# A hybrid attention and mLSTM model: the plain step's rotation in tiles of its own, and another order of the last pair's scores, exchange and weight splits

## The chip, the cores and the metric

The kernel runs on one core of a Trainium2 chip. The core has five engines: PE (TensorE, matmuls into PSUM), DVE (VectorE), ACT (ScalarE), POOL (GpSimd, here mostly a queue that issues DMAs) and SP (SyncE, a queue that issues DMAs). Each engine takes its instructions in order from its own queue, and waits on semaphores for the others. The metric is the device time of one execution in microseconds.

## The reference, cut to what matters

Two layers over a sequence of 512 tokens with 1024 features: dilated attention with a SwiGLU, then an mLSTM with a SwiGLU. The change lies in the attention layer alone.

```python
DIL_CONFIGS = ((128, 1), (512, 4), (2048, 16))     # 3 groups: window, dilation
ATTN_HEADS, ATTN_HEAD_DIM, ROT_DIM = 8, 128, 32

def dilated_attention_mixer(xn, positions, w_in, w_out):
    proj = (xn @ w_in).reshape(B, S, N_GROUPS, 3, ATTN_HEADS, ATTN_HEAD_DIM)
    scale = ATTN_HEAD_DIM ** -0.5
    for g, (window, dilation) in enumerate(DIL_CONFIGS):
        q = apply_partial_rope(proj[:, :, g, 0], positions) * scale   # rotates 32 of 128 features
        k = apply_partial_rope(proj[:, :, g, 1], positions)
        v = proj[:, :, g, 2]
        o, lse = dilated_window_attention(q, k, v, window, dilation)
        outs.append(o); lses.append(lse)
    wts = jax.nn.softmax(jnp.stack(lses), axis=0)                     # one softmax over the groups
    o = jnp.einsum('gbsh,gbshd->bshd', wts, jnp.stack(outs))
    return o.reshape(B, S, ATTN_WIDTH) @ w_out

def reference(...):
    h = x
    h = h + dilated_attention_mixer(rms_norm(h, attn_norm[0]), positions, attn_w_in[0], attn_w_out[0])
    h = h + swiglu(rms_norm(h, ffn_norm[0]), ffn_w_in[0], ffn_w_out[0])
    h = h + mlstm_mixer(rms_norm(h, mlstm_norm[0]), ...)
    h = h + swiglu(rms_norm(h, ffn_norm[1]), ffn_w_in[1], ffn_w_out[1])
    return rms_norm(h, final_norm)
```

## The kernel before

**Matmuls in three passes.** Every large operand is split in a high and a low part, and a product is made of three matmuls: high by high, high by low, low by high (`SPLITS`). A weight chunk of 128x1024 (or a block difference) is loaded on SP's queue into a `wraw` buffer, its high part is copied by ACT (L217) and its low part is subtracted by DVE (L219), both in `split_chunk`. A `Feed` makes the chunks in the order of a plan, two, later three, ahead of the one in use: what a chunk's preparation issues is traced three chunks before PE needs it. Activations are split the same way by `split_act` (L233 on ACT, L234 on DVE).

**Order of the work.** The program is traced once, and a compile-time planner then orders each engine's queue: of the instructions that its own timing has ready it takes the one traced first. An edge from `tc.issue_after(ins)` keeps an instruction behind `ins` on the same engine. `run` does this for PE on both sides, so that a piece of work stands as one block between two others. `defer(n, fn)` traces a piece of work n steps later, where `advance()` is called at the end of a step. `behind_scores` holds the low splits and the block differences behind `ahead_of_splits`, the last reduction of the latest plain scores.

**Attention, pair by pair.** The 8 heads are done in 4 pairs (`pr` 0 to 3), each in three groups `g`. In pairs 1 to 3 group 0 is the plain step (`project_pair` and `project`): query, then key, two chunks each, so four steps. Groups 1 and 2 are each a `qk_unit` of seven products of 24 matmuls in the order P1, P5, P6, P2, P7, P3, P4 (a Strassen-like scheme), with steps ending after P5, P2, P3 and P4. ACT copies partial sums out of PSUM (L885 after P1, L888 after P5, L890 after P6, L897 after P2 and P4). P7 goes on adding to the PSUM bank that L890 reads, so P7's first matmul waits for L890. P5 of the next group waits for a bank that L897 of P4 reads last.

**Rotation.** 32 of the 128 features of each query and key are packed into one tile of 128 partitions (`rot`, tag "rot", one buffer), by ACT (L965 in the plain step, L879 `pack` in the units). `rope` turns them on DVE (L598 to L607), and its `back` copies them back on ACT: 8 copies at L613 in the plain step, 4 at L615 in the units. The last unit (pair 3, group 2) adds straight into the query and key (L604). The plain step's `back` is deferred by one step, into the next unit, after its P5.

**Scores, softmax and values.** `scores0` does the plain group's scores (L691), masks and reduces them on DVE (L697) and takes exponentials on ACT (L732); it is deferred by 6 steps (`SCORES0_AT`) from the end of the plain step, so it stands in group 2 behind P2. `scores12` does groups 1 and 2 (L713, L716, L738), one step into the next pair. `joint` exchanges the maxima and sums between the groups' orders of the tokens (a matmul, L751) and makes the factors; `weigh` multiplies them in (L783, L786), `transposes` turns a head's weights over (L792) and stores them to memory with four DMAs on POOL (L795), `bring` loads them back (L800, on POOL, in the last pair on SP), and `values` multiplies by the values (L810, L815). `RUN_AT` holds the steps for all that: scores of groups 1 and 2, the rest (joint with the first head's weighing, its transposes, the second head's weighing, its transposes with the first load, the second load), the two heads' values, and the loads of the values. PSUM has two banks for each head's scores, "s" and "o", and the values use "o" too; `keep_head` (L627) copies a head's output out of it.

**After the last pair** follows a wide product of the values of groups 1 and 2 (`project_tokens_wide`, L331: four chunks of 24 matmuls, each in four blocks of tokens), with the last pair's scores after its first chunk and its joint work amid the third (`amid=(2, 1)`), all of it by `LAST_AT`. The heads kept in memory come back (`bring_heads`, L634), four of them are split (L233, L234), and the output projection begins (`out_part`, L249), with the last pair's values put between its parts.

Of the kernel before, what the change touches and what calls it, by code (L numbers as in the profile page):

```python
# [17 lines left out]
P = 128  # L18
# [55 lines left out]
def tile_hybrid_dilated_attn_mlstm(  # L74
# [132 lines left out]
    def behind_scores():  # L207
        return tc.issue_after(ahead_of_splits[0]) if ahead_of_splits[0] is not None else nullcontext()
    splits = itertools.count()

    def split_chunk(chunk):

        raw, n, view, name = chunk
        p, more, bufs = (spare[0], "4", 1) if spare and next(splits) % (W_BUFS + 1) == W_BUFS else (wp, "", W_BUFS)
        hi = p.tile([P, 1024], F32R, tag="whi" + more, name=name + "_h", bufs=bufs)
        lo = p.tile([P, 1024], F32R, tag="wlo" + more, name=name + "_l", bufs=bufs)
        nc.scalar.activation(hi[:, :n], raw[:, :n], AF.Copy)  # L217
        with behind_scores():
            nc.vector.tensor_tensor(lo[:, :n], raw[:, :n], hi[:, :n].bitcast(F32), op=ALU.subtract)  # L219
        return view(hi), view(lo)  # L220
# [174 lines left out]
    with ExitStack() as actx:  # L395
# [194 lines left out]
        def packed(rot, q, m, blocks):  # L590
            a = rot[quarter(q), 0, m * HALF:(m + 1) * HALF]
            return a.rearrange("p (c b j) -> p b c j", c=2, b=TB) if blocks else a

        def rope(qk, rot, blocks, first=0, end=4, direct=False):

            at = slice(R * first, R * end)
            a, sh = rot[at, 0], rot[at, 1]
            nc.vector.stream_shuffle(sh, a, shift)  # L598
# [3 lines left out]
            if direct:  # L602
                for q in range(first, end):
                    nc.vector.tensor_tensor(halves(qk[q // 2][:R], q % 2), two_m(rot[quarter(q), 0]),  # L604
                                            two_m(rot[quarter(q), 1]), op=ALU.add)
                return
            nc.vector.tensor_tensor(a, a, sh, op=ALU.add)  # L607

            def back():
                for q in range(first, end):  # L610
# [3 lines left out]
                    else:  # L614
                        nc.scalar.activation(halves(qk[q // 2][:R], q % 2), two_m(rot[quarter(q), 0]), AF.Copy)  # L615
            return back
# [28 lines left out]
        def attention_pair(pr, qks):  # L645
# [58 lines left out]

            def scores12(qk1, qk2):

                banks_ = {}
                for g, (q, k) in ((1, qk1), (2, qk2)):
                    for i in range(2):
                        sp = banks_[g, i] = score_bank(i, "%ss%d" % (nm, g))  # L710
                        for c in range(4):
                            sl = slice(c * P, (c + 1) * P)
                            nc.tensor.matmul(sp[:, sl], q[:, i, sl], k[:, i, sl], start=True, stop=True)  # L713
                for g, i in ((1, 0), (2, 0), (1, 1), (2, 1)):
                    for c in range(4):
# [112 lines left out]
            if pr == HEADS // 2 - 1:  # L828
                rest = (lambda: (first_rest(), transposes(0), weigh(1), transposes(1)),)
            return (lambda: (places(), scores0(*qks[0])), lambda: scores12(*qks[1:]), rest, values, load_values,  # L830
                    value_tiles, bring)

# [37 lines left out]
        def qk_unit(pr, g, qk):  # L870
# [7 lines left out]
            def pack(q, src):  # L878
                nc.scalar.activation(two_m(rot[quarter(q), 0]), src, AF.Copy)  # L879

            def finish(name):
# [9 lines left out]
                elif name in ("P2", "P4"):  # L891
                    th = int(name == "P4")
                    src = two_m(acc[target[name]])
                    if th == 0:
                        rot = ap.tile([P, 2, SEQ], F32, tag="rot", name="rot")
                    pack(th, src[:R])
# [39 lines left out]
        def project_pair(pr, qks, then=None):  # L936
            nm = "a%d" % pr
            for g in range(3):
# [10 lines left out]
                def rot(box=box):  # L949
                    if not box:  # L950
                        box.append(ap.tile([P, 2, SEQ], F32, tag="rot", name="rot"))
                    return box[0]
                for part in range(2):
# [24 lines left out]
                    if part == 1:  # L978
# [1360 lines left out]
```

## Time and profile before

| | |
|---|---|
| three runs | 1401.36, 1401.41, 1396.04 us (median 1401.36) |
| profiled execution | 1398.08 us |
| its span | 1396.3 us, mean granted clock 0.997 |
| pairs 1 to 3 | about 180 to 415 us of the span |
| wide values and first output projection | about 415 to 485 us |

The times lie within 0.4% of each other. The span runs from the first to the last profiled instruction, and the execution's own time is 1.8 us longer. Busy time by stretch (us from the start; PE, weight loads, DVE, ACT, POOL busy, then the granted clock of PE, the DMA share and GB/s):

```
180.00:260.00 80.00, 79.24 (x557) 74.14 (x556) 63.67 (x155) 54.11 (x125) 11.50 (x21) 1.00 0.58 169
260.00:340.00 80.00, 77.37 (x547) 72.35 (x546) 60.15 (x138) 50.78 (x111) 10.97 (x19) 1.00 0.53 156
340.00:415.00 75.00, 72.93 (x520) 69.03 (x519) 58.95 (x136) 45.07 (x99) 7.36 (x14) 0.98 0.56 172
415.00:485.00 70.00, 65.33 (x333) 54.44 (x332) 36.48 (x99) 26.71 (x67) 7.72 (x14) 1.00 0.50 157
```

In each stretch PE is the engine with the least idle time. A row of the timeline reads: start, length, engine, line of the kernel, operation, tile written and tiles read, shape and count, and in brackets the idle time of that engine just before it with what ended it.

### The profile page before, as it was taken

How to read it: one execution, taken by the hardware profiler on the slowest of the kernel's cores; microseconds unless marked ns; L12 is line 12 of the kernel's file. 1: busy time of each engine (PE TensorE's matmuls, PEld its weight loads, DVE VectorE, ACT ScalarE, POOL GpSimd, SP SyncE). 2: the span in 40 equal slices, each digit the busy share in tenths (PEclk: the TensorE clock that was granted, in tenths of full speed). 3: DMA queues.
4: the chain of work that ended last, by engine and by line, in shares of the span. 5: the costliest groups of instructions: out<-in, count | busy, mean ns of one | idle time of the engine just before them, and what ended most of it. 6: DMA issues, size and time to landing. Idle time of an engine off the chain costs nothing. (4 is left out here: it accounts for less than half of the span.)

```text
span 1396.3 us, 22650 instructions
## 1 busy us (share of the span) xinstructions
PE 1372.7 (98%) x8740; PEld 1245.1 (89%) x8740; DVE 1110.8 (80%) x1853; ACT 797.5 (57%) x1334; POOL 163.2 (12%) x240
## 2 busy tenths in 40 slices
PE   9999999999999999999999999999999999999997
PEld 7888889889897789999999998898888899999886
DVE  7768679596878289877887898898858987888887
ACT  6556566666655255444467464785535544458854
POOL 3000011111011000000000100123201230001213
PEclk9999999999999999999999999999999999999999
DMA  9534246547384446333353733324334563335963
GB/s 299 172 121 136 90 138 201 155 123 232 88 258 140 157 133 163 112 121 121 98 159 77 167 121 93 91 76 112 100 112 115 139 187 122 121 107 133 198 166 99
DMA packets 140069, 193.82 MB, mean 139 GB/s; under 512 B 8981, under 2 KB 104789, under 8 KB 139961
## 3 DMA queue, kind: packets, MB, share of 16 engines
q1 hardware_dynamic: 119552, 139.81, 32.1%
q0 software_dynamic: 18752, 51.43, 15.8%
q8 instruction: 69, 1.13, 0.3%
q10 hardware_dynamic: 1656, 1.12, 0.2%
q14 instruction: 40, 0.32, 0.1%
HBM read 167.30 MB, written 22.54 MB: 136 GB/s over the span
## 5 line engine op out<-in xcount | busy, mean ns | idle before, releaser
L1642 POOL DMA_DIRECT2D f1T<-in_ffn_w_out_dram x15 | 17.8, 1185 | 209.1 <-DMA f1P_2w_w<-in_ffn_w_out_dram 136.7
L1617 POOL DMA_DIRECT2D f0S<-in_ffn_w_out_dram x10 | 8.7, 874 | 259.9 <-DVE f0hid L1534 173.0
L2174 POOL DMA_DIRECT2D hD<-hB x32 | 21.7, 696 | 68.5 <-DVE hB L2171 68.5
L249 PE MATMUL mo<-n_h,mo_k_l 128*128 128x512 f32 x64 | 25.3, 396 | 0.0
L249 PE MATMUL mo<-n_h,mo_k_h 128*128 128x512 f32 x64 | 25.2, 394 | 0.0
L249 PE MATMUL awo<-ao_h,awo_k_h 128*128 128x512 f32 x64 | 25.2, 393 | 0.0
L249 PE MATMUL mo<-n_l,mo_k_h 128*128 128x512 f32 x64 | 25.1, 393 | 0.0
L249 PE MATMUL mwo<-yo_l,mwo_k_h 128*128 128x512 f32 x64 | 25.1, 393 | 0.0
L249 PE MATMUL mqk<-n_h,mqk_k_h 128*128 128x512 f32 x64 | 25.1, 392 | 0.0
L249 PE MATMUL mqk<-n_l,mqk_k_h 128*128 128x512 f32 x64 | 25.1, 391 | 0.0
L249 PE MATMUL awo<-ao_l,awo_k_h 128*128 128x512 f32 x64 | 25.0, 391 | 0.0
L249 PE MATMUL f1j<-n_h,f1j_h 128*128 128x512 f32 x64 | 25.0, 391 | 0.0
L249 PE MATMUL f0j<-n_h,f0j_h 128*128 128x512 f32 x64 | 25.0, 391 | 0.0
L249 PE MATMUL mqk<-n_h,mqk_k_l 128*128 128x512 f32 x64 | 25.0, 390 | 0.0
L249 PE MATMUL mwo<-yo_h,mwo_k_l 128*128 128x512 f32 x64 | 25.0, 390 | 0.0
L249 PE MATMUL awo<-ao_h,awo_k_l 128*128 128x512 f32 x64 | 25.0, 390 | 0.0
L249 PE MATMUL f0j<-n_h,f0j_l 128*128 128x512 f32 x64 | 24.9, 390 | 0.0
L249 PE MATMUL f1j<-n_h,f1j_l 128*128 128x512 f32 x64 | 24.9, 390 | 0.0
L249 PE MATMUL f0j<-n_l,f0j_h 128*128 128x512 f32 x64 | 24.9, 389 | 0.0
L249 PE MATMUL f1j<-n_l,f1j_h 128*128 128x512 f32 x64 | 24.9, 389 | 0.0
L249 PE MATMUL mwo<-yo_h,mwo_k_h 128*128 128x512 f32 x64 | 24.9, 391 | 0.0
L219 DVE TENSOR_TENSOR v1P_l<-v1W,v1P_h 128x1024 fp32r<-128x1024 f32 x14 | 17.1, 1224 | 9.3 <-ACT v1P_h L217 9.3
(2617 smaller groups left out, 5891.9 us busy)
## 6 DMA issues: line engine op xcount, KB each, us to landing
f0j_w<-in_ffn_w_in_dram SPq DMA_DIRECT2D x17, 512.0 KB, 5.4
f1j_w<-in_ffn_w_in_dram SPq DMA_DIRECT2D x17, 512.0 KB, 6.1
f1T<-in_ffn_w_out_dram POOLq DMA_DIRECT2D x15, 512.0 KB, 6.5
f0hid<-in_ffn_w_in_dram SPq DMA_DIRECT2D x9, 512.0 KB, 5.7
f1hid<-in_ffn_w_in_dram SPq DMA_DIRECT2D x9, 512.0 KB, 5.3
v0W<-in_attn_w_in_dram SPq DMA_DIRECT2D x8, 512.0 KB, 7.2
v1W<-in_attn_w_in_dram SPq DMA_DIRECT2D x8, 512.0 KB, 4.4
awo_k_w<-in_attn_w_out_dram SPq DMA_DIRECT2D x8, 512.0 KB, 6.0
```

The costliest lines, as they stand in the source:

```text
L219: nc.vector.tensor_tensor(lo[:, :n], raw[:, :n], hi[:, :n].bitcast(F32), op=ALU.subtract)
L249: nc.tensor.matmul(acc, whl[a][:, k, m * P:(m + 1) * P], pairs[b][kk], start=(kk == 0 and (a, b) == SPLITS[0]), stop=(kk == nk - 1 and (a, ...
L1617: nc.gpsimd.dma_start(t, src[1][:, ks], accum_op=ALU.add)
L1642: nc.gpsimd.dma_start(view(to), weight_rows(hk * UNITS + u, n), accum_op=ALU.add)
L2174: nc.gpsimd.dma_start(hD[k // 4].rearrange("(b i) x -> i b x", i=R)[:, :, c0:c0 + R], t[R * a_:R * (a_ + 1)])
```

## The change

It does six things.

1. In pairs 1 to 3 the plain step's rotation gets two tiles of its own (tags "rbc" and "ssum" of the norm pool, which that stage doesn't use otherwise) in place of the one "rot" buffer that the units use, and its copies back are deferred by 3 steps instead of 1, so behind P3 of group 1.
2. In pair 3 the plain scores come one step sooner (5 in place of 6, behind P5 of group 2), and so do the second head's weighing, its transposes and both loads of pair 2's weights (`RUN3_AT`).
3. The last pair's scores of group 1 are done at once after pair 3, ahead of the wide values; those of group 2 in the middle of the first chunk (`amid=(0, 1)`).
4. The last pair's exchange, factors, first head's weighing and transposes are one piece, traced after the second chunk; the second head's weighing and transposes follow behind the splits of the four heads.
5. From that piece on, low splits stand behind the first head's weighing on DVE (`ahead_of_splits`) and high splits behind the exponential of the factors on ACT (`ahead_of_casts`, `behind_factors`), to the end of the attention layer.
6. The splits of the heads 2 and 3, and of 4 and 5, are held in the same way.

```diff
-SCORES0_AT = 6
+SCORES0_AT = (None, 6, 6, 5)
 RUN_AT = (1, (4, 5, 8, 8, 9), (11, 12), (2, 3, 1))
-LAST_AT = (1, (3, 3, 3, 3, 3), (), (1, 1, 1))
+RUN3_AT = (1, (4, 5, 7, 7, 8), (11, 12), (2, 3, 1))
+LAST_AT = (1, (2,), (), (1, 1, 1))
...
+    ahead_of_casts = [None]
+
+    def behind_factors():
+        return tc.issue_after(ahead_of_casts[0]) if ahead_of_casts[0] is not None else nullcontext()
...
-        nc.scalar.activation(hi[:, :n], raw[:, :n], AF.Copy)
+        with behind_factors():
+            nc.scalar.activation(hi[:, :n], raw[:, :n], AF.Copy)
...
-            a, sh = rot[at, 0], rot[at, 1]
+            a, sh = rot[0][at], rot[1][at]
...
-            def scores12(qk1, qk2):
-
-                banks_ = {}
-                for g, (q, k) in ((1, qk1), (2, qk2)):
+            banks_ = {}
+
+            def scores12(gs=(1, 2)):
+
+                for g in gs:
+                    q, k = qks[g]
...
-                for g, i in ((1, 0), (2, 0), (1, 1), (2, 1)):
+                for g, i in [e for e in ((1, 0), (2, 0), (1, 1), (2, 1)) if e[0] in gs]:
...
             if pr == HEADS // 2 - 1:
-                rest = (lambda: (first_rest(), transposes(0), weigh(1), transposes(1)),)
+                def all_rest():
+                    first_rest()
+                    ahead_of_splits[0] = last_on(DVE)
+                    ahead_of_casts[0] = last_on(ACT)
+                    transposes(0)
+                rest = (all_rest,)
+
+            def second():
+                weigh(1)
+                transposes(1)
...
                 def rot(box=box):
                     if not box:
-                        box.append(ap.tile([P, 2, SEQ], F32, tag="rot", name="rot"))
-                    return box[0]
+                        if pr:
+                            box.extend(npl.tile([P, SEQ], F32, tag=tag, name="rot") for tag in ("rbc", "ssum"))
+                        else:
+                            t = ap.tile([P, 2, SEQ], F32, tag="rot", name="rot")
+                            box.extend((t[:, 0], t[:, 1]))
+                    return box
...
-                            defer(1, turn())
+                            defer(3 if pr else 1, turn())
...
-            defer(at[0], lambda: run(scores12_))
+            defer(at[0], lambda: run(scores12_ if at is not LAST_AT else lambda: scores12_((2,))))
...
-            follow(todo, RUN_AT)
-            project_pair(pr, qks, lambda fn=following[0]: defer(SCORES0_AT, lambda: run(fn)))
+            follow(todo, RUN3_AT if pr == 3 else RUN_AT)
+            project_pair(pr, qks, lambda fn=following[0], pr=pr: defer(SCORES0_AT[pr], lambda: run(fn)))
             todo = following
         last_values, last_bring = todo[3], todo[6]
+        run(lambda: todo[1]((1,)))
         follow(todo, LAST_AT)
...
-                            amid=(2, 1))
+                            amid=(0, 1))
         pair = x_tiles("ao")
         for k in range(4):
-            split_act(pair[0][k], pair[1][k], o_head(k), None)
+            with behind_scores() if k > 1 else nullcontext(), behind_factors() if k > 1 else nullcontext():
+                split_act(pair[0][k], pair[1][k], o_head(k), None)
+        behind(todo[7], engine=DVE)
...
                 last_bring(c - 1, nc.sync)
-                split_act(pair[0][3 + c], pair[1][3 + c], o_head(3 + c), None)
+                with behind_scores():
+                    split_act(pair[0][3 + c], pair[1][3 + c], o_head(3 + c), None)
...
         spare.clear()
+        ahead_of_splits[0] = ahead_of_casts[0] = None
```

The other lines of the diff carry the two tiles through `packed`, `rope`, `back` and `pack`.

More of the change, by code (lines that the diff above doesn't have):

```diff
@@ L590, in packed @@
         def packed(rot, q, m, blocks):
-            a = rot[quarter(q), 0, m * HALF:(m + 1) * HALF]
+            a = rot[0][quarter(q), m * HALF:(m + 1) * HALF]
             return a.rearrange("p (c b j) -> p b c j", c=2, b=TB) if blocks else a
@@ L603, in rope @@
                 for q in range(first, end):
-                    nc.vector.tensor_tensor(halves(qk[q // 2][:R], q % 2), two_m(rot[quarter(q), 0]),
-                                            two_m(rot[quarter(q), 1]), op=ALU.add)
+                    nc.vector.tensor_tensor(halves(qk[q // 2][:R], q % 2), two_m(rot[0][quarter(q)]),
+                                            two_m(rot[1][quarter(q)]), op=ALU.add)
                 return
@@ L614, in back @@
                     else:
-                        nc.scalar.activation(halves(qk[q // 2][:R], q % 2), two_m(rot[quarter(q), 0]), AF.Copy)
+                        nc.scalar.activation(halves(qk[q // 2][:R], q % 2), two_m(rot[0][quarter(q)]), AF.Copy)
             return back
@@ L828, in attention_pair @@
             if pr == HEADS // 2 - 1:
-                rest = (lambda: (first_rest(), transposes(0), weigh(1), transposes(1)),)
-            return (lambda: (places(), scores0(*qks[0])), lambda: scores12(*qks[1:]), rest, values, load_values,
-                    value_tiles, bring)
+                def all_rest():
[7 more added lines that the diff above has]
+                transposes(1)
+            return (lambda: (places(), scores0(*qks[0])), scores12, rest, values, load_values,
+                    value_tiles, bring, second)
         postponed = []
@@ L878, in pack @@
             def pack(q, src):
-                nc.scalar.activation(two_m(rot[quarter(q), 0]), src, AF.Copy)
+                nc.scalar.activation(two_m(rot[0][quarter(q)]), src, AF.Copy)
             def finish(name):
```

3 lines of the change are left out of this document (2 added, 1 removed).

## The prediction

> **What bounds the kernel now.** I read the page's busy times first, then the waits of PE by four stretches from 140 to 480 us (engine, line, what it waited for; total us, times, longest us), then the timeline around each of those waits.
>
> ```profile
> PE 1372.7 (98%) x8740; PEld 1245.1 (89%) x8740; DVE 1110.8 (80%) x1853; ACT 797.5 (57%) x1334; POOL 163.2 (12%) x240
> ```
>
> ```profile
> PE a1g1u L923 <- ACT a1g1vu L890: 0.8, 1, 0.8
> PE a2g1u L923 <- ACT a2g1vu L890: 2.1, 1, 2.1
> PE a2g2p L923 <- ACT a2g_q L897: 0.6, 1, 0.6
> PE a3g1u L923 <- ACT a3g1vu L890: 2.1, 1, 2.1
> PE a3o L810 <- DMA a3pT<-a3pD: 2.4, 1, 2.4
> PE a3s L713 <- DVE a3g_q L604: 1.0, 1, 1.0
> PE a3g12v L331 <- ACT a3g_q L897: 0.7, 1, 0.7
> PE a3xps L751 <- DVE a3ex L746: 0.6, 1, 0.6
> ```
>
> PE sets the end: it is busy 98% of the span. The change removes no matmul, so it can only win PE's waits. All eight waits above lie in the attention layer, and they sum to 0.8+2.1+0.6+2.1+2.4+1.0+0.7+0.6 = 10.3 us. The other waits of PE are outside the edited code.
>
> A wait costs more than its idle time. The timeline (start us, length us, engine, line, operation, [idle before, releaser]) around the one in pair 2:
>
> ```profile
> 293.63 0.28 PE L923 MATMUL a2g1c<-xa_h,a2g1P_l 128*128 128x256 f32 x1
> 295.98 0.38 PE L923 MATMUL a2g1u<-S3h,a2g1P_h 128*128 128x256 f32 x1 [2.08 <-ACT a2g1vu L890]
> 296.20 0.28 PE L923 MATMUL a2g1u<-S3l,a2g1P_h 128*128 128x256 f32 x1
> ```
>
> A stream of these matmuls starts one every 0.12 us (380.15 and 380.27 below). Without the wait the row at 296.20 would have started at 293.87, so 2.33 us are lost, 0.25 more than the idle time. Eight waits make that 2.0 us. The same wait in pair 3 has a second price:
>
> ```profile
> 378.00:380.00 2.00, 2.00 (x12) 2.00 (x11) 2.00 (x3) 0.26 (x1) 0.00 (x0) 0.50 0.98 175
> ```
>
> ```profile
> 376.97 0.41 PE L923 MATMUL a3g1u<-S3h,a3g1P_h 128*128 128x256 f32 x1
> 377.18 0.41 PE L923 MATMUL a3g1u<-S3l,a3g1P_h 128*128 128x256 f32 x1
> ...
> 380.15 0.28 PE L923 MATMUL a3g1p<-S4h,a3g1P_h 128*128 128x256 f32 x1
> 380.27 0.28 PE L923 MATMUL a3g1p<-S4l,a3g1P_h 128*128 128x256 f32 x1
> ```
>
> The granted clock is 0.50 in that stretch, matmuls start 0.21 us apart instead of 0.12, and full speed is back by 380.15. About 3.2 us at 0.12/0.21 of the pace lose 1.4 us. Around pair 2's equal wait, and around that of 2.4 us, the windows grant 1.00. So the ceiling of the change is 10.3+2.0+1.4 = 13.7 us.
>
> The Trainium skill ("TensorE: Matmul & The Clock Gate", Part 1) has the clock fall to half after an idle window of about 3.4 us, and warns of gaps above some 3 us. By it a 2.07 us wait costs no clock, and the ceiling would be 12.3 us; the rows above differ, and the measurement decides.
>
> **Part 1: the plain step's rotation (pairs 1 to 3).** ACT in pair 2:
>
> ```profile
> 292.53 1.46 ACT L613 ACTIVATE a2g_q<-rot 32x256 f32<-32x256 f32 x4 [2.86 <-DVE rot L607]
> 294.00 1.45 ACT L613 ACTIVATE a2g_k<-rot 32x256 f32<-32x256 f32 x4
> 295.36 0.57 ACT L890 ACTIVATE a2g1vu<-a2g1u 128x512 f32<-128x512 f32 x1
> ```
>
> Eight copies (2.9 us) wait for the rotation's last add and stand ahead of L890, which P7's matmuls need. The change traces them two steps later, behind P3, and gives this rotation two tiles of its own, so that P2's pack into "rot" doesn't wait for them. It adds and removes no instruction. L890 can then run when P6 ends, before P2 does, hidden under P2's 24 matmuls. The copies go into ACT's idle time and are needed only by the scores in group 2, some 20 us later; without that cover they cost 2.9 us again.
>
> What is late next? Group 2's P5 and P2:
>
> ```profile
> 304.63 1.22 DVE L853 TENSOR_TENSOR a2g2W<-a2g2W,a2g2W 128x1024 f32<-128x1024 f32 x1 [0.62 <-DMA a2g2W<-in_attn_w_in_dram]
> 313.00 1.21 DVE L219 TENSOR_TENSOR a2g2P_l<-a2g2W,a2g2P_h 128x1024 fp32r<-128x1024 f32 x1
> ```
>
> ```profile
> 305.95 1.06 ACT L217 ACTIVATE a2g2P_h<-a2g2W 128x1024 fp32r<-128x1024 f32 x1 [1.27 <-DVE a2g2W L853]
> 307.65 0.60 ACT L897 ACTIVATE a2g_q<-a2g1u 128x512 f32<-128x512 f32 x1
> ```
>
> ```profile
> 314.40 0.28 PE L923 MATMUL a2g2c<-xa_h,a2g2P_l 128*128 128x256 f32 x1
> 317.04 3.20 PE L691 MATMUL a2s<-a2g_k,a2g_q 128*128 128x128 f32 x16
> ```
>
> P5 waits until L897 ends at 308.25, and L897 stands behind the split L217, which waits for DVE, which waits for a weight load. P2's low part ends at 314.21, 0.19 us before its first use, and from 304.63 on DVE has no idle time ahead of it. The change moves neither in pairs 1 and 2, so most of a gain in pair 2 is a later wait. In pair 3 the plain scores (L691, 16 matmuls in about 2.8 us) move to one step earlier, ahead of P6 and P2, and cover P2's split; the weighing and transposing of pair 2's second head, with its four stores and a load on POOL's queue, one step earlier too, leave DVE's path before it, while the stores share the DMA engines with that weight load. Terms:
>
> - Pair 1: at most 0.8+0.25 = 1.0, at least 0; I take 0.5, the middle, since nothing here decides.
> - Pair 2: at most 2.08+0.56+0.5 = 3.1, at least 0; I take 0.7, near the 0.19 of slack.
> - Pair 3: at most 2.07+0.25+1.4 = 3.7, at least 0 (P5's chain); I take 2.3, the wait without the clock, which is chance.
>
> **Part 2: the last pair.** Now:
>
> ```profile
> 409.97 1.06 ACT L217 ACTIVATE a3g12v_k_h<-a3g12v_k_w 128x1024 fp32r<-128x1024 f32 x1 [7.42 <-DMA a3g12v_k_w<-in_attn_w_in_dram]
> 417.55 0.60 ACT L627 ACTIVATE o_keep<-a2o 128x512 f32<-128x512 f32 x1
> 418.05 1.06 ACT L217 ACTIVATE a3g12v_k_h<-a3g12v_k_w 128x1024 fp32r<-128x1024 f32 x1
> 419.74 0.60 ACT L897 ACTIVATE a3g_q<-a3g2u 128x512 f32<-128x512 f32 x1
> ```
>
> ```profile
> 415.33 0.48 PE L331 MATMUL a3g12v<-a3g12v_k_h,xa_h 128*128 128x512 f32 x1
> 420.39 0.50 PE L331 MATMUL a3g12v<-a3g12v_k_h,xa_h 128*128 128x512 f32 x1 [0.70 <-ACT a3g_q L897]
> 425.27 1.60 PE L713 MATMUL a3s<-a3g_k,a3g_q 128*128 128x128 f32 x12 [0.99 <-DVE a3g_q L604]
> ```
>
> Group 1's 16 scores (0.13 us each by the last row, 2.1 us) move to 415.33, ahead of the wide values; group 2's go behind two of the first chunk's four blocks, the exchange behind the second chunk instead of amid the third. The plain exponentials, traced two units of 24 matmuls (5.8 us) sooner, can use the 7.42 us in which ACT waits for a weight load; now they run after it and hold up the copies up to L897. That would free the waits of 0.7, 1.0 and 0.6 (3.0 with 0.25 for each restart). The softmax chain starts some 5 us sooner (425.27 against 420.2, below), and with it the exchange through memory, whose loads stand on SP's queue so:
>
> ```profile
> 457.64 0.37 SPq L201 DMA_DIRECT2D f0j_w<-in_ffn_w_in_dram  x1
> 458.24 1.04 SPq L800 DMA_DIRECT2D a3pT<-a3pD  x1
> 463.59 0.36 SPq L800 DMA_DIRECT2D a3pT<-a3pD  x1
> ```
>
> ```profile
> DMA to landing us min/median/max: 7.7/7.7/7.7
> ```
>
> ```profile
> 466.06 1.80 PE L810 MATMUL a3o<-a3pT,a3v 128*128 128x128 f32 x14 [2.38 <-DMA a3pT<-a3pD]
> ```
>
> The first load stands behind a weight load that waits for a buffer until 457.64. Issued 5 us sooner it lands near 461, before PE asks at 463.7: 2.6 us gone. Late next is the second one, behind another such weight load: it lands at 463.59+7.7 = 471.3, and PE asks at 466.06+3.3 (values)+2.8 (12 wide matmuls, those of 415.33 at 0.23 us) = 472.2. The 0.9 us between them don't cover 2.6, so 1.7 come back unless this load too passes the weight load on SP. Part 3, the splits held behind the factors (ACT) and the weighing (DVE), costs nothing in itself: it lets the chain pass 1.2 us splits. Behind the held splits wait SP's refills of their buffers and the output projection, which has its first chunk ready and needs each next one 24 matmuls (5.5 us) later. The loads of the last values, on POOL, come half a chunk sooner, behind the store of o_keep; PE needs them at 466. The second head's weighing now also waits for the splits of four heads on DVE. The other end: the scores of group 2 need a q that is ready at 425.27 now, and PE would ask at 415.33+2.1+2.8 = 420.2. If that chain doesn't move, this wait grows from 1.0 to 5.1. So the part lies between +5.6 (3.0+2.6) and -4.1; I take 3.9 (3.0+2.6-1.7), since freeing ACT feeds the first three waits.
>
> Sum: 0.5+0.7+2.3+3.9 = 7.4 us off the profiled execution of 1398.08 (span 1396.3), so 1390.7. That execution lies within the runs shown (1396.04 to 1401.41), 3.3 us below their median. Three waits of 2 us or more can each meet a half-clock stretch of 1.4 us, and the profiled run met one. If the median run met all three (an estimate from these rows), the change is worth 7.4+2*1.4 = 10.2 there: 1391.2. From both I predict 1391.
>
> **Rivals.**
> *The stall only moves* (0.17). In every pair P5's chain, weight load to L853 to L217 to L897, keeps PE at today's start, and DVE at P2. For it: the slack of 0.19 us and L897 behind a waiting split. Against it: in pair 3 the moved scores cover P2. Then the pairs give 0 and the last pair its 3.9: 1394.2.
>
> *The copies stay* (0.08). The compiler's planner issues what is ready; the copies are ready at 292.5 with ACT idle for 2.86 us, so they may stand before L890 still. Part 2 is left, with less of it, since ACT stays as full: 3.0, so 1395.1.
>
> *Slower: the last q is late* (0.20). ACT takes its queue in order, and a split waits in it for weights:
>
> ```profile
> 412.80 0.49 ACT L732 ACTIVATE a3p<-a3p,a3nb 128x256 f32<-128x256 f32 x1
> ```
>
> If the copies of P4 (L897) stay behind the split at 418.05, group 2's scores wait 4.1 us more, a wait long enough for a half-clock stretch (1.4). Group 1's second head needs a PSUM bank that o_keep at 417.55 frees at 418.15: with one head's scores done at 416.4, PE waits 1.8. L890 in pair 3's group 2 may queue behind the sooner exponentials: eight at 0.49 are 3.9 us, its own copy 0.57, P2 covers 2.9, so 1.6. The late load adds 1.7. With nothing won in the pairs that is 10.6: 1408.7. For it: ACT idle 7.42 us behind such a split today. Against it: without the exponentials ACT reaches L897 before those weights land, so the planner may put it first. It decides where L897 falls against that split.
>
> **How the numbers follow.** Forecast 0.55, the rivals 0.17, 0.08, 0.20. A measurement here tells 0.5%, 7 us, from no change. The forecast is 7.4 to 10.2 us: faster, but for a tenth of its chance. The middle rivals (3 to 4 us, or up to 7 against a run with more half-clock stretches) are mostly no change and give 0.07 to faster. The last rival is slower, but for a tenth of it. That is faster 0.57, same 0.25, slower 0.18. The range runs from 1384.4 (the ceiling, 1398.1-13.7) to 1405, which leaves out most of the slower rival; the forecast's own is 1385 to 1396.
>
> **What would show it.** Right: no PE wait on L890 in group 1; ACT's copies of L613 later than P2's L879; pair 3's plain exponentials before 409; no wait of 2 us at a3o. Wrong: PE waits at group 2's P5 or P2 (on L897, L219) of what L890's cost; a wait of several us at a3s on L604 or on its bank.

## The result, and the profile after

The changed kernel takes 1403.11 us (median of 14 runs, 1401.43 to 1405.88), the kernel before 1399.57 us in the same comparison (14 runs, 1396.04 to 1401.41). The ratio is 1.0027, with a 95% interval of 1.0019 to 1.0036: 3.5 us slower, where 10 us faster was forecast. By the prediction's bound of 0.5% this is no change; its sign is nonetheless clear.

The profiled execution of after has a span of 1401.2 us, 4.9 more than that of before, and the same work on PE: 1373.2 us against 1372.7. So nearly the whole difference is idle time of PE again. Its waits in the attention layer (the view of the waits, in stretches from 140 to 500 us; columns as in the prediction; a3g2p is pair 3, group 2 and one of the unit's sums, a3s are the scores of pair 3 and a3o its values):

```profile
PE a1g1u L942 <- ACT a1g1vu L908: 0.4, 1, 0.4
PE a2g1u L942 <- ACT a2g1vu L908: 1.1, 1, 1.1
PE a1g2p L942 <- ACT a1g_q L916: 1.0, 1, 1.0
PE a2g2p L942 <- ACT a2g_q L916: 0.7, 1, 0.7
PE a2g1u L942 <- DVE a2g_k L923: 0.6, 1, 0.6
PE a3g2p L942 <- DVE a3g2P_l L226: 5.5, 1, 5.5
PE a3g2p L942 <- ACT a3g_q L916: 2.0, 1, 2.0
PE a3g1u L942 <- ACT a3g1vu L908: 0.6, 1, 0.6
PE a3g1u L942 <- DVE a3g_k L923: 0.6, 1, 0.6
PE a3o L819 <- DMA a3pT<-a3pD: 1.6, 1, 1.6
```

The lines have moved: L908 is L890 of before, L916 is L897, L897 is L879, L226 and L224 are the splits L219 and L217, L704 is L697, L942 is the matmul line L923, L923 is now the key's add (L904), and L620 are the copies back (L613). Before had 5.6 us in the pairs and 4.7 in the last pair, 10.3 in all; after has 12.5 and 1.6, 14.1 in all. The last pair won 3.1 us. The waits on L890 went from 5.0 to 2.1, but new ones came behind them: on P4's copy of q (L916, 3.7 where 0.6 stood), on the key's add (L923, 1.2), and one of 5.5 us that before had no trace of. The sums differ by 3.8 us and the medians by 3.5. Each of the two profiles has one stretch at half the granted clock in these stages (0.59 at 376 to 380 us before; 0.69 and 0.88 at 408 to 412 and 412 to 416 after), so that this price doesn't tell them apart.

Where that long wait lies, the two stretches that were shown of before read after the change:

```profile
340.00:415.00 75.00, 66.29 (x455) 61.72 (x454) 57.01 (x137) 46.34 (x104) 8.06 (x14) 0.98 0.52 156
415.00:485.00 70.00, 68.36 (x386) 59.22 (x385) 37.57 (x98) 25.33 (x59) 7.71 (x14) 1.00 0.56 176
```

PE was busy for 72.93 and 65.33 us in them; now for 66.29 and 68.36. The timeline of after around the wait, in order of start:

```profile
398.54 1.06 ACT L224 ACTIVATE a3g2P_h<-a3g2W 128x1024 fp32r<-128x1024 f32 x1 [0.21 <-PE a3g2u L942]
403.36 1.06 ACT L224 ACTIVATE a3g12v_k_h<-a3g12v_k_w 128x1024 fp32r<-128x1024 f32 x1 [3.28 <-DMA a3g12v_k_w<-in_attn_w_in_dram]
404.32 0.57 ACT L897 ACTIVATE rot<-a3g2c 32x512 f32<-32x512 f32 x1
404.94 0.01 DVE L605 LOAD_MASK_SELECT rot<-rot  x1 [8.42 <-ACT rot L897]
406.29 0.27 DVE L704 CUSTOM_DVE_ANT_0 a3p<-a3s,acst 128x128 f32<-128x128 f32 x1
408.43 0.41 DVE L704 CUSTOM_DVE_ANT_0 a3p<-a3s,acst 128x256 f32<-128x256 f32 x1
408.85 1.21 DVE L226 TENSOR_TENSOR a3g2P_l<-a3g2W,a3g2P_h 128x1024 fp32r<-128x1024 f32 x1
410.11 0.58 PE L942 MATMUL a3g2p<-S4h,a3g2P_l 128*128 128x256 f32 x1 [5.50 <-DVE a3g2P_l L226]
```

Read it from the bottom. PE waits for P3's low split, which DVE starts at 408.85, though its high part was cast before 399.6. Directly ahead of it stand the eight reductions of the plain scores (406.29 to 408.85), ahead of those q's rotation, ahead of that P2's pack on ACT (404.32), and ahead of that a cast of the wide values' first chunk, for which ACT stood 3.28 us because its weights had not landed. DVE, which takes its queue in order, did nothing for 8.42 us until the pack came. In the kernel before, the same split of P3 ran at 396.92 and that of P4 at 398.92, and the plain reductions followed at 402.83:

```profile
396.92 1.22 DVE L219 TENSOR_TENSOR a3g2P_l<-a3g2W,a3g2P_h 128x1024 fp32r<-128x1024 f32 x1
398.92 1.23 DVE L219 TENSOR_TENSOR a3g2P_l<-a3g2W,a3g2P_h 128x1024 fp32r<-128x1024 f32 x1 [0.78 <-ACT a3g2P_h L217]
402.83 0.27 DVE L697 CUSTOM_DVE_ANT_0 a3p<-a3s,acst 128x128 f32<-128x128 f32 x1
```

### The profile page after: what moved, and what is told of

It is laid out like the page before. It is cut to its first block, busy times and chain, and to the rows that moved or that the text cites. A ratio compares the mean times of both kernels' runs of the same rounds, so it can differ in the third digit from the quotient of the medians.

```text
span 1401.2 us, 22635 instructions
## 1 busy us (share of the span) xinstructions
PE 1373.2 (98%) x8740; PEld 1245.5 (89%) x8740; DVE 1110.8 (79%) x1853; ACT 798.4 (57%) x1334; POOL 163.3 (12%) x240
## 5 line engine op out<-in xcount | busy, mean ns | idle before, releaser
L226 DVE TENSOR_TENSOR v1P_l<-v1W,v1P_h 128x1024 fp32r<-128x1024 f32 x14 | 17.1, 1223 | 9.3 <-ACT v1P_h L224 9.3
```

## The experiments

**The theories.** The first (H): the cause is an edge. `behind_scores` keeps every low split that is traced after the plain scores behind their last reduction. With the scores one step sooner, the splits of P3 and P4 are traced after them and not before, so they are held. Its rivals: the late cast in front of P2's pack is the cause, or the weights that land late for it because the sooner loads of the transposed weights share the DMA engines, or the time was lost in the last pair. For the pairs the rival M says that a stall that goes at L890 only moves to the next unit. Twelve kernels were run in three groups; the kernel before had medians of 1398.93, 1399.38 and 1399.16 us in these groups (33 to 35 runs each), and each ratio is to the kernel before of the same group. Waits in us, of one profiled execution each:

| kernel | median us (runs) | ratio to before [95%] | waits, pairs | waits, last pair |
|---|---|---|---|---|
| before | 1399.57 (14) | | 5.6 | 4.7 |
| after | 1403.11 (14) | 1.0027 [1.0019, 1.0036] | 12.5 | 1.6 |
| pair 3's sooner steps undone | 1399.9 (11) | 1.0012 [1.0002, 1.0022] | 6.0 | 6.0 |
| first wide cast behind P2's pack | 1400.52 (12) | 1.0011 [1.0002, 1.0021] | 11.0 | 1.4 |
| splits of P3 and P4 not held | 1397.63 (11) | 0.9992 [0.9983, 1.0001] | 8.1 | 1.5 |
| pair 3's transposes later | 1401.12 (11) | 1.0017 [1.0008, 1.0026] | 11.8 | 1.0 |
| rotation alone | 1399.23 (11) | 0.9998 [0.9989, 1.0007] | 5.6 | 4.5 |
| last pair's part alone | 1400.56 (11) | 1.0014 [1.0004, 1.0024] | 6.7 | 6.3 |
| not held, transposes later | 1401.28 (11) | 1.0013 [1.0003, 1.0022] | 8.0 | 3.7 |
| not held, no rotation part | 1398.07 (12) | 0.9992 [0.9982, 1.0002] | 8.6 | 3.1 |
| not held, copies back behind P3 | 1398.74 (11) | 0.9996 [0.9987, 1.0006] | 7.9 | 1.2 |
| not held, a bank for P5 | 1398.31 (11) | 0.9996 [0.9988, 1.0005] | 6.4 | 3.4 |
| all of these edges | 1396.81 (11) | 0.9989 [0.998, 0.9998] | 4.8 | 6.0 |
| all of these edges, transposes later | 1397.79 (12) | 0.9998 [0.9987, 1.0008] | 5.4 | 7.2 |

### Which link of the chain costs the 5.5 us

**Splits not held.** The low splits of pair 3's P3 and P4 are taken out of the edge, and nothing else is changed.

```diff
-        with behind_scores():
+        with nullcontext() if name in ("a3g2P3", "a3g2P4") else behind_scores():
             nc.vector.tensor_tensor(lo[:, :n], raw[:, :n], hi[:, :n].bitcast(F32), op=ALU.subtract)
```

> The changed kernel with the low splits of P3 and P4 in pair 3's group 2 not held behind the plain scores. Theory H: P3's low split runs when its high part ends (398.3), the 5.5 us wait goes and with its restart the time falls to about 1397.3. Rival (DVE's own order, the rotation that waits for ACT, stands ahead of it anyway): the wait and the 1403 stay.

The wait at P3 is gone, and the median falls by 5.5 us to 1397.63 (ratio 0.9992 in place of 1.0027; against the kernel before of each comparison that is 1.3 us faster in place of 3.5 us slower, so 4.8 us). The waits in the table fall by 4.5 us, since the values of pair 2 and the exchange now wait 1.1 us each. The timeline of this kernel has both splits at 399.00, long before P2's pack, although the late cast is still there:

```profile
399.00 2.38 DVE L226 TENSOR_TENSOR a3g2P_l<-a3g2W,a3g2P_h 128x1024 fp32r<-128x1024 f32 x2 [1.83 <-ACT a3g2P_h L224]
404.03 1.06 ACT L224 ACTIVATE a3g12v_k_h<-a3g12v_k_w 128x1024 fp32r<-128x1024 f32 x1 [3.43 <-DMA a3g12v_k_w<-in_attn_w_in_dram]
405.00 0.57 ACT L897 ACTIVATE rot<-a3g2c 32x512 f32<-32x512 f32 x1
```

The cast waits 3.43 us and the pack runs at 405.00, later than in after, and PE does not wait. So the edge is the cause, and the rest of the chain matters only through it.

**First wide cast behind P2's pack.** After, with the wide values' casts kept behind P2's copies on ACT.

```diff
                 finish(name)
+                if last and name == "P2":
+                    ahead_of_casts[0] = last_on(ACT)
```

> The changed kernel with one more order edge: from P2 of pair 3's group 2 on, high splits stand behind P2's copies on ACT, so the first split of the wide values, which waits for its weights until 403.3, no longer stands ahead of P2's pack. If that late load alone makes the wait (rival), the 5.5 us at a3g2p go and the time is about 1397.5. Theory H: DVE gets P2's pack about 2 us sooner, the split stays behind the plain scores, so the wait falls to 3 to 3.5 us and the time to about 1401.

The chain now runs from the pack at 403.18 without the cast, which comes at 406.19, and PE's wait falls from 5.5 to 3.4:

```profile
403.18 0.59 ACT L897 ACTIVATE rot<-a3g2c 32x512 f32<-32x512 f32 x1 [1.51 <-PE a3g2c L942]
408.35 1.21 DVE L226 TENSOR_TENSOR a3g2P_l<-a3g2W,a3g2P_h 128x1024 fp32r<-128x1024 f32 x1
409.61 0.39 PE L942 MATMUL a3g2p<-S4h,a3g2P_l 128*128 128x256 f32 x1 [3.41 <-DVE a3g2P_l L226]
```

The pack is as early as PE lets it be here (it waits for P2's product), and still 3.4 us remain: from the pack to the split lie a shuffle, two products and eight reductions, 5.2 us, with only P7's 24 matmuls (2.9 us) to cover them. The held split loses even with nothing late in front of it. The cast adds 2.1 us.

**Pair 3's transposes later.** After, with `RUN3_AT` as `RUN_AT`, so that the transposed weights are loaded later.

```diff
-RUN3_AT = (1, (4, 5, 7, 7, 8), (11, 12), (2, 3, 1))
+RUN3_AT = (1, (4, 5, 8, 8, 9), (11, 12), (2, 3, 1))
```

> The change with pair 3's transposes and weighted rows back in their old steps (RUN3_AT as RUN_AT) and the plain scores still one step sooner. H (the held split is the cause, and the sooner transposes make it worse through the wide value weights, which share the DMA engines with them): the first wide weights land 3.7 to 5.1 us after their issue as before, not 6.0 to 6.3, P2's pack starts about 402.3 instead of 404.3, the wait on P3's low split falls from 5.5 to about 3.5 us, time 1400.5 to 1401.5. D (the landing does not depend on the transposes): the wait stays 5 to 6 us, time 1402.5 to 1403.5.

Half of this came as expected and half did not. The timeline of this kernel:

```profile
401.28 1.06 ACT L224 ACTIVATE a3g12v_k_h<-a3g12v_k_w 128x1024 fp32r<-128x1024 f32 x1 [1.73 <-DMA a3g12v_k_w<-in_attn_w_in_dram]
402.24 0.57 ACT L897 ACTIVATE rot<-a3g2c 32x512 f32<-32x512 f32 x1
405.01 0.68 DVE L611 TENSOR_TENSOR a3g_q<-rot 32x512 f32<-32x512 f32 x1
405.62 0.27 DVE L704 CUSTOM_DVE_ANT_0 a3p<-a3s,acst 128x128 f32<-128x128 f32 x1
409.44 0.58 PE L942 MATMUL a3g2p<-S4h,a3g2P_l 128*128 128x256 f32 x1 [5.50 <-DVE a3g2P_l L226]
```

The cast waits 1.73 us for its weights in place of 3.28 and the pack runs 2.1 us sooner, so the sooner transposes do delay those weights (two further pairs of kernels below agree: 3.43 against 1.39 us with the splits not held, 4.28 against 0.98 with all the edges). But the wait of PE stays at 5.5: the planner now put all of q's rotation (up to L611) ahead of the reductions, two operations more than in after, which took 1.4 us, and PE came 0.7 us sooner. Freed time in front of a held instruction was filled with other work that was ready. The time of 1401.12 us lies in the expected band, but not for the reason given: the wait did not shrink. What did shrink are the waits at P5 (L916, from 2.0 to 0.9) and at the transposed weights (from 1.6 to 1.0); with 0.4 more at L908 that is 1.3 of the 2.0 us.

### The pairs: what the rotation's part is worth

**Rotation alone.** The kernel before with only item 1's tiles and copies back (the other constants and orders as before).

```diff
-                        box.append(ap.tile([P, 2, SEQ], F32, tag="rot", name="rot"))
+                        if pr:
+                            box.extend(npl.tile([P, SEQ], F32, tag=tag, name="rot") for tag in ("rbc", "ssum"))
...
-                            defer(1, turn())
+                            defer(3 if pr else 1, turn())
```

> The kernel before with the rotation's part alone (two tiles of its own, copies back traced 3 steps later). Theory M (the planner leaves 2 to 8 of the copies ahead of L908, and what is won there comes back at P4, at group 2's P5 and P2): waits in pairs 1 to 3 of about 6.0 us against 5.6 before, the last pair as before, so 1399 to 1400, no change. Rival, the forecast of the prediction: 2 to 3.5 us won in the pairs, 1396.

Nothing changes: 0.9998 [0.9989, 1.0007], and the waits in the pairs sum to 5.6 us, as before. They only have other names; its three largest:

```profile
PE a2g1u L942 <- ACT a2g1vu L908: 1.1, 1, 1.1
PE a3g1u L942 <- ACT a3g1vu L908: 1.0, 1, 1.0
PE a1g2p L942 <- ACT a1g_q L916: 0.8, 1, 0.8
```

Two things keep the gain away. The first is on ACT in pair 2 (timeline of after; this kernel has the same order):

```profile
294.09 1.46 ACT L620 ACTIVATE a2g_q<-rot 32x256 f32<-32x256 f32 x4 [2.87 <-DVE rot L614]
295.57 0.41 ACT L620 ACTIVATE a2g_k<-rot 32x256 f32<-32x256 f32 x1
295.89 0.57 ACT L908 ACTIVATE a2g1vu<-a2g1u 128x512 f32<-128x512 f32 x1
```

Five of the eight copies, 1.9 us, still stand ahead of L908 in pairs 2 and 3 (four in pair 1); only the others went behind it. They are traced two steps later, but in the planner's own timing they are ready while ACT has nothing else, so it issues them. The second is that PE, when it comes sooner, waits at P4 and at the next unit's P5 instead.

**Copies back behind P3's pack** (on top of the splits not held): the copies are tied to their place by an edge.

```diff
-                            defer(3 if pr else 1, turn())
+                            defer(3 if pr else 1, (lambda b=turn(): behind(b, engine=ACT)) if pr else turn())
```

> The kernel whose P3 and P4 splits aren't held, with an order edge that puts the eight copies back behind P3's pack on ACT in pairs 1 to 3, so that none stands ahead of L908. Both theories: no PE wait on L908 in group 1 (0.4, 1.1 and 1.0 us now). Theory M: the sum of the waits in pairs 1 to 3 stays within 1 us of its 7.0, on L916, L923 or L226 instead, and the time within 1 us of 1397.6. Rival: 2.5 us and three restarts won, 1394.4.

All waits on L908 are gone, and PE waits as long as ever, one unit later. The three long ones of this kernel in the pairs:

```profile
PE a2g2p L942 <- ACT a2g_q L916: 2.6, 1, 2.6
PE a1g2p L942 <- ACT a1g_q L916: 2.3, 1, 2.3
PE a3g2p L942 <- ACT a3g_q L916: 2.3, 1, 2.3
```

What P5 of group 2 waits for, on ACT in pair 3:

```profile
386.57 1.46 ACT L620 ACTIVATE a3g_q<-rot 32x256 f32<-32x256 f32 x4
388.04 1.46 ACT L620 ACTIVATE a3g_k<-rot 32x256 f32<-32x256 f32 x4
391.21 0.60 ACT L916 ACTIVATE a3g_q<-a3g1u 128x512 f32<-128x512 f32 x1
```

The same eight copies, 2.9 us, now stand in front of P4's copies, which free the bank of P5. This is M, on the spot.

**A bank for P5.** The splits not held, the first wide cast behind P2's pack, and P5's sum in a PSUM bank of its own, so that it need not wait for P4's copies. **All of these edges** adds the tie of the copies.

```diff
-                    acc[key] = acc_tile(nm + key)
+                    acc[key] = acc_tile(nm + key) if name == "P1" else ps.tile([P, 512], F32, tag="t", name=nm + key, bufs=1)
```

> The kernel whose P3 and P4 splits aren't held, with the first split of the wide values behind P2's pack on ACT as well, and with P5's sums in the PSUM bank of tag t, which pairs 1 to 3 don't use, so that group 2's P5 doesn't wait for the bank that L916 of P4 reads. If that bank is what the stall moved to: the waits at g2p on L916 (1.1, 0.4, 1.8) go, the a2o and a3xps waits (1.1 each) shrink, 1397.6-4.5 = 1393. If DVE's split of P2 (0.2 us of slack) is as late (theory M's last step): waits on L226 take their place and the time is 1396 to 1397.

> The kernel with the bank for P5 and the copies back behind P3's pack as well. If the stalls of the pairs are each of its own: no wait on L908 and L916, 1390 to 1392. Theory M: P2's and P6's low splits on DVE take what is won, 1394 to 1396.

The waits on L916 go, and those in the pairs fall from 8.1 to 6.4 and then 4.8 us. But the last pair's grow from 1.5 to 3.4 and 6.0, spread over the bank that o_keep frees, the last q, the exchange and the transposed weights.

All three kernels missed the gain of several us that was forecast for removing their waits: 1398.74, 1398.31 and 1396.81. They also lie 0.1, 1.3 and 0.8 us above the bands that were expected by M. In the last two the waits that M named, on L226, are 0.6 and 1.7 us; the others that came stand on further copies of ACT (L622, L903 and L908 of group 2). With all the edges the median is 2.6 us below that of before, with an interval that just misses 1. After twelve kernels an interval that close is not called a gain; its profile sums to 10.8 us of waits, no less than before.

**Not held, no rotation part.** The last pair's part and pair 3's sooner steps, with the rotation's tile and copies as before.

```diff
-                        if pr:
+                        if False:
                             box.extend(npl.tile([P, SEQ], F32, tag=tag, name="rot") for tag in ("rbc", "ssum"))
...
-                            defer(3 if pr else 1, turn())
+                            defer(1, turn())
```

> P3's and P4's low splits not held, and the rotation's part of the change left out (tile and copies back as before): the last pair's part and pair 3's sooner steps alone. If the rotation's part is worth something once the held split is gone, its waits of before return (a1g1u 0.8, a2g1u 2.1, a3g1u 2.1 us on the copy L908, a2g2p 0.6) and the new ones go (L916 at a1g2p 1.1, a2g2p 0.4; L923 0.6): 5.6 us against 3.6 us, time 1398.5 to 1400. If it only moves stalls (M): 1397 to 1398.

1398.07, with the same ratio of 0.9992 as with the rotation's part. The waits of 0.8, 2.1 and 2.1 us on L908 are back, and the sum in the pairs is 8.6 us where 5.6 were expected: P5 of pair 3 waits 2.6 us, which the expectation didn't count, and 0.6 stays at P5 of pair 1, which was to go. Between the two bands that were expected the time lies at the edge of M's. The rotation's part is worth nothing that these runs can tell, by itself or with the rest.

### The last pair: what its gain needs

**Pair 3's sooner steps undone.** After, with the plain scores of pair 3 at step 6 again and `RUN3_AT` as `RUN_AT`.

```diff
-SCORES0_AT = (None, 6, 6, 5)
+SCORES0_AT = (None, 6, 6, 6)
-RUN3_AT = (1, (4, 5, 7, 7, 8), (11, 12), (2, 3, 1))
+RUN3_AT = (1, (4, 5, 8, 8, 9), (11, 12), (2, 3, 1))
```

> The changed kernel with pair 3's plain scores back at 6 steps and pair 2's second head back at the old steps (the earlier steps of pair 3 undone, all else kept). Theory H (the plain scores one step sooner put P3's low split of pair 3, group 2, behind them, and that costs the 5.5 us wait): the waits of 5.5 and most of 2.0 us at a3g2p go, those of pairs 1 and 2 stay; 1403.1-7.5 = 1395.6, some 4 us below the kernel before. Rival (the last pair's new order or the rotation costs the time): no gain, 1401 to 1403.

**The last pair's part alone.** That kernel, with the rotation's tile and copies back as before too (the edits of the two diffs above together).

> The kernel before with the last pair's part alone (scores of group 1 at once, group 2's amid the first chunk, joint sooner, splits held; rotation and pair 3's steps as before). If that part wins what it wins in the changed kernel by itself (waits of 0.7, 1.0 and 0.6 gone, a3o 2.4 to 1.6): 3.1 us idle and three restarts of 0.25, so 1399.6-3.9 = 1395.7, with pairs 1 to 3 as before. If it needs pair 3's sooner scores (rival): group 2's scores wait for their q, some 5 us at a3s, and the time is 1400 to 1404.

In both the wait at P3 is gone, as H has it, since the splits are traced before the scores again. But the last pair's waits rise to 6.0 and 6.3 us. Both kernels miss the gain that H and the last pair's own worth had them forecast (1395.6 and 1395.7); the second lies in its rival's band, the first below it. Their ratios lie 0.12% and 0.14% above 1. The part alone, on PE:

```profile
PE a3s L722 <- ACT o_keep L634: 1.6, 1, 1.6
PE a3s L722 <- DVE a3g_q L611: 3.3, 1, 3.3
```

These are the two waits of the prediction's slower rival, the bank that o_keep frees (1.8 forecast) and the last q (from 1.0 to 5.1 forecast). Neither shows in after. So the gain of the last pair isn't its own: without the sooner steps nothing is won. That it is a loss is not shown, since the lower ends of the intervals, 1.0002 and 1.0004, are about as close to 1 as the interval that was called no gain above.

**Not held, transposes later** separates the two sooner steps: plain scores at 5, P3 and P4 free, transposes in the old steps.

> P3's and P4's low splits not held, and pair 3's transposes back in their old steps. H: the wait on P2's copy of q (1.8 us with the transposes sooner) falls below 1 us, the wait for the transposed weights before the values (0.4 us) may grow to 1.5 us: 1396.5 to 1397.5, no clear gain over the run with the splits not held (1397.6). D: nothing changes, 1397.6.

The wait at P5 fell from 1.8 to 1.0 us, as expected, but the time rose by 3.7 us to 1401.28, against both expectations. A wait of 3.4 us on the last q (L611) is back. On ACT it comes about so:

```profile
412.99 1.06 ACT L224 ACTIVATE a3g12v_k_h<-a3g12v_k_w 128x1024 fp32r<-128x1024 f32 x1 [6.84 <-DVE a3g_k L923]
413.95 0.38 ACT L741 ACTIVATE a3p<-a3p,a3nb 128x128 f32<-128x128 f32 x1
421.29 0.59 ACT L897 ACTIVATE rot<-a3g2u 32x512 f32<-32x512 f32 x1
```

The eight plain exponentials stand behind a cast for which ACT is idle for 6.84 us, and P4's pack comes at 421.29. With the transposes sooner (the kernel with the splits not held) the exponentials begin at 411.53 and the pack at 418.25:

```profile
411.53 0.39 ACT L741 ACTIVATE a3p<-a3p,a3nb 128x128 f32<-128x128 f32 x1
418.25 0.59 ACT L897 ACTIVATE rot<-a3g2u 32x512 f32<-32x512 f32 x1
```

The 3.0 us at the pack are most of the wait. What ends the idle 6.84 us is the key's add on DVE (L923); why that comes later isn't traced further. So with the splits not held the last pair needs the sooner transposes. Whether it needs the sooner scores, which are what held the splits, isn't shown: no kernel has the sooner transposes without them. With the splits held, the later transposes leave the last pair 1.0 us of waits (the table), since PE then comes late from the stall of 5.5 us.

**All of these edges, transposes later**, with `RUN3_AT` as in the other runs:

> The best kernel so far (splits not held, first cast behind P2's pack, a bank of its own for P5, copies back behind P3's packs: 1396.8) with pair 3's transposes back in their old steps. H: the first wide weights land about 2 us sooner, so the last pair's keeping of the finished sums and last q (1.4 and 1.7 us of wait) come at most 1 us sooner: 1395.8 to 1396.8. M (the stall only moves): 1396.5 to 1397.5.

1397.79, above both bands. The first wide cast waits for its weights 0.98 us in place of 4.28, but the second one waits 7.77 in place of 3.46, the last q is ready at 425.11 in place of 423.25, and the last pair's waits grew from 6.0 to 7.2 us where they were to shrink.

## Why the prediction was wrong, point by point

- **What bounds the kernel: right.** PE's work did not change (1373.2 against 1372.7 us), and the time followed its waits: 3.8 us more of them, 3.5 us more time.
- **The step that failed** is pair 3's term in part 1: the plain scores one step earlier, "ahead of P6 and P2, and cover P2's split". It looked at what the moved matmuls cover on PE and not at the edge that goes with them. `behind_scores` is set by the scores' last reduction and holds every split traced after it; one step sooner means that P3's and P4's splits fall on the other side. The front part of this document says what the edge does, and the prediction priced no split behind it but the new ones of part 3, "costs nothing in itself". Price: 2.3 us of gain forecast; measured, an extra wait of 5.5 us, and about 5 us of time when the edge alone is taken off these two splits.
- **Pairs 1 and 2 (0.5 and 0.7): the size, and the rival that was set at 0.17.** The waits that were forecast to go did shrink at L890, from 2.9 to 1.5 us, and those behind it, at P5 and P4, grew from 0.6 to 2.3. The rotation alone gives 0.0 us in the pairs. The prediction named P5 as what is late next and still took a gain. The rival of the stall that only moves was right about the pairs, and so in part was that of the copies that stay: five of eight did.
- **The transposes in pair 3**: the prediction saw that they share the DMA engines with P5's weight load and gave it no price. P5 waits 2.0 and 1.8 us with them sooner (after, and with the splits not held), 0.9 and 1.0 with them later.
- **The last pair (3.9): the number right, in part by luck.** The waits of 0.7, 1.0 and 0.6 us are gone, 3.0 with their restarts as forecast. The 2.4 us at the first load are gone, and the second load, behind another weight load on SP's queue, is late by 1.6 us where 1.7 was forecast:

```profile
476.55 1.83 PE L819 MATMUL a3o<-a3pT,a3v 128*128 128x128 f32 x14 [1.64 <-DMA a3pT<-a3pD]
```

  But the first two waits are gone also because PE comes later. The prediction had PE begin group 1's scores at 415.33, the time of the wide values before; after the stall it begins them at 423.66, and the last q is ready at 426.79. With the splits not held, 1.5 us of waits are left in the last pair, yet PE begins these scores at 418.58, since the waits of the pairs rose from 5.6 to 8.1 us; the last q is ready at 423.39, 1.8 us sooner than before (425.22). Where the pairs wait less, PE comes sooner and the waits return: with a bank for P5 it begins the scores at 416.62 and the last pair waits 3.4 us, with all the edges at 414.82 and 6.0 us, while q is ready at 423.17 and 423.25. The prediction added the terms of the pairs and of the last pair as if each stood alone; these runs show that a part of them is one stall in two places. Nor did it see that the last pair's term rests on pair 3's sooner steps, without which its own slower rival comes true (1.6 and 3.3 us).
- **What would show it.** Of the four signs that were named for being right only the last came, no wait of 2 us at a3o. PE still waits for L908 in group 1, pair 2's last copies back (297.57) stand ahead of P2's pack (299.71), and the plain exponentials of pair 3 run from 408.96 to 412.7 instead of ending before 409. The first sign for being wrong came: waits at group 2's P5 on L916, 1.0, 0.7 and 2.0 us.
- **Part 3, the held splits of the last pair**: no wait on them shows in after. Nothing was run to take them alone.
- **The slower rival had the right sign and another mechanism.** In after, neither the bank nor the last q makes a wait. The time of 1403.11 lay in the range only because that rival stretched it to 1405.

The account closes for the sum: the last pair's 3.1 us won, the pairs' 6.9 lost (5.5 of it the held split). The change with the splits not held is level with the kernel before at 0.9992 [0.9983, 1.0001], and none of the further edits is clearly better.

## What to carry to other kernels

When a piece of work that sets an ordering edge is moved, list every instruction that changes sides of the edge, and time each against its use; here two splits of 1.2 us, held behind a chain of 5 us with 2.9 us to cover it, turned a change that is level without them into one that is 0.27% slower. A wait that is taken away in a kernel whose main engine is 98% busy counts only if the next thing that engine asks for is ready as much sooner: run the edit alone before its price enters a sum. An edit that is a gain only together with another should be priced as the pair, and two waits of the main engine that hang on the same chain should be priced as one, since the first of them can hide the second.

## What the runs showed of the hardware

A wait of PE can be followed by a stretch at half the granted clock, and whether it is can't be told from its length alone. The kernel with the copies behind P3's pack has three waits of nearly one length, and the windows behind the second and the third read (columns as in the tables of stretches):

```profile
311.95 0.50 PE L942 MATMUL a2g2p<-S,a2g2P_h 128*128 128x256 f32 x2 [2.57 <-ACT a2g_q L916]
391.86 0.50 PE L942 MATMUL a3g2p<-S,a3g2P_h 128*128 128x256 f32 x2 [2.35 <-ACT a3g_q L916]
```

```profile
312.00:316.00 4.00, 4.00 (x22) 4.00 (x23) 4.00 (x7) 2.31 (x3) 2.73 (x5) 0.59 0.59 128
392.00:396.00 4.00, 4.00 (x31) 3.90 (x32) 4.00 (x6) 3.35 (x5) 1.18 (x3) 1.00 0.94 233
```

Behind the wait of 2.57 us the clock is 0.59 in the mean over 4 us; behind that of 2.35 it is 1.00. Over the fourteen profiles of this study (attention layer), 6 of the 14 waits of 2.0 to 2.7 us and 5 of the 6 of 3.2 us or more were followed by such a stretch; no window of 4 us granted less than 0.97 without one of these waits before it. The Trainium skill ("TensorE: Matmul & The Clock Gate", Part 1) puts the drop behind an idle window of about 3.4 us; the waits of 2.0 to 2.7 us that were followed by one are shorter than that.

The traces also tell which waits are followed by one. In windows of 0.2 us each such stretch is 3.41 us long at 0.50 (one, with pair 3's transposes later, is twice that), and two in one run start a whole number of such lengths apart: in the kernel above at 230.83 and 312.75 us, which is 24 times 3.413, and in the kernel before at 376.69 and, near the end of the run, 1390.45, which is 297 times 3.413. So the run of each kernel can be divided into cells of 3.413 us that begin or end with its own stretch (with pair 3's sooner steps undone the only one lies near the end, at 1393.49). The 20 waits leave PE idle for 2.00 us or more of one cell twelve times, and each time the next cell is at half clock; no cell of which they take 1.87 us or less is followed by one. The wait of 2.57 us lies in one cell; that of 2.35 is divided into 1.75 and 0.60. What the runs show is thus a bound between 1.87 and 2.00 us of idle time in a cell, and not the length of the wait alone. Where the cells lie differs from run to run, so for a forecast it stays chance: a wait above 2 us can cost some 1.4 us more than its length (an estimate from the prediction's rows), and a kernel whose waits all stay under 2 us, as with the splits not held, has none of it.
